# Small products of several sequences issued in turn, and copies shared out anew, in a hybrid attention step

## The chip, the cores and the metric

The kernel runs on one core of a Trainium2 chip. A core has five engines with a queue each: TensorE (PE in the profile, its weight loads PEld), VectorE (DVE), ScalarE (ACT), GpSimd (POOL) and SyncE (SP), which issues most DMAs. An engine takes the instructions of its queue in order. The metric is the device time of one execution in microseconds, lower is better.

## What is computed

One step of a hybrid decoder layer is run for a prompt of 1024 tokens and for a sample group of 8 sequences with 4 new tokens each, which share the weights. The part that matters here is the sparse attention of the sample group, for each of the two key/value heads:

```
kcmp, vcmp = compress(k), compress(v)      # 127 block summaries of the 2048 cached rows
lc  = q . kcmp * scale + bias;   pc = softmax(lc);   o_cmp = pc . vcmp
imp = pc . sel_map;              idx = top_k(imp, 16 blocks of 64 rows)
ls  = q . selected rows * scale + bias;   o_slc = softmax(ls) . selected values
lw  = q . window rows * scale + bias;     o_win = softmax(lw) . window values   # 512 rows
a   = g0 * o_cmp + g1 * o_slc + g2 * o_win
```

A summary is gelu(flat(block + pe) @ w1) @ w2, a small network over 32 rows at a stride of 16. Everything is float32. Behind the attention follow the merge with the short convolution, w_o, a residual, a squared-ReLU MLP and a final norm.

## The kernel before

Large products are split into a high and a low part in a faster float32 format (`mm3`, three products each, lines 212 to 214). The small products of the sample attention are plain float32, which the array runs as two passes each.

The work of the sample group stands beside the compression of its cache. The compression handles the 16 caches (8 sequences, keys and values): the first six key caches one at a time in `sample_unit` with `comp_unit` during the prompt's attention, and the other ten two by two in `pair_unit`. A pair unit gathers the raw rows by an indirect DMA on POOL's queue, puts them in order by heads (`by_heads`, four quarters q for each sequence; q = 3 on POOL, the others on VectorE), transposes them (ct), evicts them on ScalarE (xt), and forms three sums of products (hid), for which VectorE and ScalarE prepare the differences and the two parts (dx, cth, ctl). `blocks_out` applies the gelu and the second weights (kvc) and leaves kcT or vcN.

The sample attention is a generator, `sample_group`, and each `yield` is a place where it can be left. The loop over the pair units resumes it SSTEP = (5, 4, 4) times after the three sums of each unit; what is left runs after the loop. The order on the engines is then planned by the compiler's scheduler from this order of the program, with its own estimate of times.

`sample_group` treats two groups of four sequences. Each sequence's queries are 32 columns (2 heads, 4 query heads, 4 tokens), so a product has 32 stationary columns, and the sequence j of a group writes the PSUM rows 32j to 32j + 31. For each group, `weights`:
- loads four window keys (`swn`, two buffers) and transposes each (`flipped`: four PE transposes into one of two PSUM tiles skT, one eviction into one of five tiles skt);
- forms the products with the summaries and the new keys (sn, lines 1133 to 1135) and with the windows (sw, line 1142), the softmaxes, the importance and the choice of blocks (im, sel);
- takes, for each half of the cached rows, the four gathered tiles (`gk`, four buffers, 512 KB each, fetched by `gather_half` on POOL's queue) one sequence after another: two flips of four tiles, each followed by its product (sl, line 1192), the eviction of the first on VectorE and that of the second on ScalarE, then `fetch()` for the next gather and a yield; then the mask is added into L;
- takes the softmax, the window values (sv, line 1113), and transposes the weights in five parts, which go to DRAM (sl_d).

`values` reads them back and forms the products with the gathered values, eight for each sequence and half (so, line 1231), those with the summaries and the new values (lines 1244 and 1245), and puts the result into the rows of aT, from which the merge (na) goes on.

Of the kernel before, what the change touches and what calls it, by code (L numbers as in the profile page):

```python
# [11 lines left out]
F32 = mybir.dt.float32  # L12
# [60 lines left out]
SSTEP = (5, 4, 4)  # L73
# [46 lines left out]
def tile_hybrid_step(ctx, tc, xp, xs, cck, ccv, csk, csv, swk, swv, sconv, ptab, g_attn, w_in,  # L120
# [317 lines left out]
    kcT = mp.tile([128, NB, 127], F32, name="kcT")  # L438
# [48 lines left out]
    def blocks_out(kv, x, t, n, b):  # L487
# [11 lines left out]
        if kv == "k":  # L499
# [8 lines left out]
            else:  # L508
                for h in range(2):
                    for mt in range(2):  # L510
                        PE.matmul(po[h * 64:h * 64 + 64, :nblk], w2[:, mt, 0, :], xh[:, mt, :nblk, h],
                                  start=mt == 0, stop=mt == 1)
                V.tensor_copy(kcT[:, b, :], po[:, :nblk])
# [12 lines left out]
    def comp_unit(kv, w1, cv, n, b):  # L526
# [60 lines left out]
        x, t = (mp.tile([128, 2, 256], F32, name=nm, tag=nm, bufs=1) for nm in ("gx", "gt"))  # L587
        for mt in range(2):
            S.activation(x[:, mt, :nv], hv[:, mt, :nv], AF.Identity, bias=pb[:, mt:mt + 1])
# [39 lines left out]
    def by_heads(raw, q):  # L629
# [3 lines left out]
        if q in GPRP:  # L633
            P.tensor_scalar(dst, src, 1.0, 0.0, op0=OP.mult, op1=OP.add)
        else:
            V.tensor_copy(dst, src)
# [6 lines left out]
    def pair_unit(kv, cache, b0, w1):  # L643
# [5 lines left out]
        for q in range(4):  # L649
            xt = u2.tile([128, 2, 512], F32, name="xt", tag="xt", bufs=XTB)  # L650
            for s_ in range(2):
                part = by_heads(raws[s_], q)
# [7 lines left out]
        x = u2.tile([128, 2, 512], F32, name="gx2", tag="gx2", bufs=1)  # L660
        xo = x.rearrange("p m (j e h) -> p m j e h", e=2, h=2)
# [426 lines left out]
    CN, CC, CS = 127, 0, 131  # L1088
    new_rows = {}

    def sample_group():
# [13 lines left out]
        def window_values(pw, rows, bs, ow):  # L1105
            pt = flipped([pw[:, i * 128:(i + 1) * 128] for i in range(4)], S.copy)
            po3 = ps(HT["sx"], "sv")
            for j, b in enumerate(bs):
                nat = s1.tile([128, 4, 128], F32, name="swn", tag="swn", bufs=SWB)
                DMA.dma_start(nat, swv[0, b].rearrange("(k p) h d -> p k (h d)", p=128))  # L1110
                keep_window(s_wv[0, b], nat)
                for i in range(4):
                    PE.matmul(po3[rows[j], :128], pt[:, i * 128 + 32 * j:i * 128 + 32 * j + 32], nat[:, i, :],
                              start=i == 0, stop=i == 3)
            V.tensor_copy(ow, po3[:, :128])

        def weights(grp):
# [14 lines left out]
            for r, b in zip(rows, bs):  # L1132
                PE.matmul(po2[r, CC:CC + 127], qb[b], kcT[:, b, :], start=True, stop=True)
                PE.matmul(po2[r, CN:CN + 4], qb[b], newT[:, 1, b * 4:b * 4 + 4], start=True, stop=True)
                PE.matmul(po2[r, CS:CS + 4], qb[b], newT[:, 0, b * 4:b * 4 + 4], start=True, stop=True)
            sn = s1.tile([128, 136], F32, name="snc", tag="snc")
            V.tensor_copy(sn[:, :135], po2[:, :135])
# [3 lines left out]
            for r, b, kt in zip(rows, bs, kts):  # L1141
                PE.matmul(po[r, :], qb[b], kt, start=True, stop=True)
# [43 lines left out]
            for half in range(2):  # L1186
                pl = [ps(HT["sx"], "sl") for _ in range(2)]
                for j, b in enumerate(bs):
                    g = gathered.pop(0)
                    for l in range(2):  # L1190
                        kt = flipped([g[:, i * 128:(i + 1) * 128] for i in range(4 * l, 4 * l + 4)], (V.tensor_copy, S.copy)[l])
                        PE.matmul(pl[l][rows[j], :], qb[b], kt, start=True, stop=True)  # L1192
                    fetch()
                    yield
                for l in range(2):
                    c = slice((2 * half + l) * 512, (2 * half + l + 1) * 512)
                    V.tensor_add(L[:, c].rearrange("p (l k c) -> p l k c", l=4, c=4),
                                 pl[l].rearrange("p (l k c) -> p l k c", l=4, c=4), selb)
# [10 lines left out]
            for q in range(5):  # L1209
                kt = flipped([L[:, i * 128:(i + 1) * 128] for i in range(4 * q, 4 * q + 4)] if q < 4 else [pc_, mx],  # L1210
                             S.copy if q % 2 else V.tensor_copy)
# [4 lines left out]
        def values(grp, ow):  # L1216
# [7 lines left out]
            for half in range(2):  # L1224
                pl = [weights_T(2 * half + i, 512) for i in range(2)]
                oo = ps(HT["sx"], "so")
                for j, b in enumerate(bs):
# [618 lines left out]
```

## Time and profile before

| | us |
|---|---|
| median of 3 runs | 1945.8 (1941.43 to 1947.84) |
| the profiled execution | 1940.09 |
| its span, first to last instruction | 1938.0 |

The profile is of one execution. Its page gives the busy time of each engine over the span; further views answer by groups of instructions (line, engine, operation, tiles written and read, shape, count, then busy time and mean ns of one, then the idle time of the engine just before them and what ended it), by stretches of time, or instruction by instruction along the timeline. In a row such as `128*32 128x512`, 128 rows and 32 columns are stationary and 512 elements of 128 partitions are moved. A matmul's time runs from its start to its modelled end, which overlaps the next one's start; what a run of them costs is read from start to start.

The whole span in 40 slices of 48.45 us, for two engines, in tenths:

```profile
PE   8999999999999999989999999999999999999998
DVE  6323332445446766758877362597766655767765
```

The pair units and the sample attention lie in the slices 18 to 23, about 858 to 1102 us.

### The profile page before, as it was taken

Reading aid. Unit: us, or ns where it says so; the run is one execution under the profiler, and the core shown is the slowest. Engines: PE = TensorE matmul, PEld = TensorE weight load, DVE = VectorE, ACT = ScalarE, POOL = GpSimd, SP = SyncE. Lnnn points to the kernel's source line nnn. Section 1 sums busy time; section 2 is a strip of 40 time slices with the busy share of each in tenths; the row PEclk is TensorE's granted clock in tenths of the full one; section 3 lists DMA queues with packets and bytes.
Section 4 is the critical chain, followed back from the end, with each engine's and each line's share of the span. In section 5 each row is a group of like instructions: output and inputs, shape, how many; then the busy total and the mean of one; then the engine's idle time right before and its main releaser. Section 6 shows DMA issues by size and latency. Waiting matters only on the chain.

```text
span 1938.0 us, 34844 instructions
## 1 busy us (share of the span) xinstructions
PE 1885.6 (97%) x13172; PEld 1753.9 (91%) x13172; DVE 1132.3 (58%) x2393; ACT 857.6 (44%) x1905; POOL 412.3 (21%) x590
## 2 busy tenths in 40 slices
PE   8999999999999999989999999999999999999998
PEld 7999999999998988876769897899999999999998
DVE  6323332445446766758877362597766655767765
ACT  5112323555555555645545221465544444544333
POOL 3112223443444443423132240020000000000000
PEclk9999999999999999999999999999999999999999
DMA  6356326212226531146546654537765666765654
GB/s 213 127 146 147 97 66 160 81 58 73 71 67 206 180 109 54 48 149 208 181 136 201 208 193 134 156 103 242 235 225 192 213 243 207 251 188 162 187 193 159
DMA packets 236312, 303.77 MB, mean 157 GB/s; under 512 B 20662, under 2 KB 163143, under 8 KB 232049
## 3 DMA queue, kind: packets, MB, share of 16 engines
q1 hardware_dynamic: 229232, 267.99, 44.3%
q0 software_dynamic: 6912, 33.56, 5.1%
q8 instruction: 104, 1.70, 0.4%
q14 instruction: 64, 0.52, 0.1%
HBM read 222.78 MB, written 78.71 MB: 156 GB/s over the span
## 4 chain that ended last, share of the span: by engine, by line
PE 84%; DMA 6%; DVE 4%; issue 3%; ACT 1%; POOL 1%; SPq 1%; DVEq 0%; POOLq 0%; ACTq 0%
PE c L213 9%; PE c L212 9%; PE c L214 9%; PE PT L939 3%; PE ga L213 3%; PE ga L212 3%; PE ga L214 3%; PE hid L213 2%; PE hid L214 2%; PE hid L212 2%; DMA wrd<-sd_d 2%; PE pv L946 2%; PE pv L945 2%; PE sl L1192 2%; PE so L1231 1%
## 5 line engine op out<-in xcount | busy, mean ns | idle before, releaser
L212 PE MATMUL c<-ud,whd 128*128 128x264 f32 x768 | 217.8, 286 | 6.2 <-ACT whd L1642 4.1
L214 PE MATMUL c<-ud,whd 128*128 128x264 f32 x768 | 217.6, 286 | 0.0
L213 PE MATMUL c<-ud,whd 128*128 128x264 f32 x768 | 217.5, 285 | 0.0
L865 POOL TENSOR_SCALAR P<-P,st,gates 128x256 f32<-128x256 f32 (+4 forms) x272 | 151.5, 577 | 118.5 <-DVE st L861 96.4
L212 PEld LDWEIGHTS c<-ud,whd 128*128 128x128 f32 x768 | 144.8, 190 | 6.8 <-ACT whd L1642 4.3
L212 PE MATMUL c<-hBt,wuh 128*128 128x264 f32 x512 | 146.3, 287 | 2.4 <-ACT hBt L1553 2.4
L214 PE MATMUL c<-hBt,wul 128*128 128x264 f32 x512 | 146.3, 286 | 0.0
L213 PEld LDWEIGHTS c<-ud,whd 128*128 128x128 f32 x768 | 145.3, 190 | 0.0
L214 PEld LDWEIGHTS c<-ud,whd 128*128 128x128 f32 x768 | 144.8, 190 | 0.0
L943 DVE TENSOR_TENSOR ptl<-PT,pth 128x512 fp32r<-128x512 f32 (+1 forms) x148 | 99.5, 686 | 66.2 <-ACT pth L942 65.8
L1642 ACT CAST whd<-wrd 128x512 fp32r<-128x512 f32 x112 | 68.3, 621 | 147.4 <-issue 97.3
L212 PE MATMUL ga<-hTh,whu 128*128 128x384 f32 (+1 forms) x384 | 127.7, 333 | 0.0
L213 PE MATMUL ga<-hTl,whu 128*128 128x384 f32 (+1 forms) x384 | 126.3, 329 | 0.0
L214 PE MATMUL ga<-hTh,wlu 128*128 128x384 f32 (+1 forms) x384 | 125.9, 328 | 0.0
L235 POOL TENSOR_TENSOR wlu<-wru,whu 128x1024 fp32r<-128x1024 f32 x32 | 76.8, 2399 | 222.6 <-ACT whu L234 222.6
L1643 DVE TENSOR_TENSOR whd<-wrd,whd 128x512 fp32r<-128x512 f32 x112 | 76.4, 690 | 79.1 <-ACT whd L1642 79.0
L942 ACT CAST pth<-PT 128x512 fp32r<-128x512 f32 (+1 forms) x148 | 83.8, 589 | 66.9 <-PE PT L939 64.2
L213 PE MATMUL c<-h2r,wuh 128*128 128x264 f32 x384 | 109.4, 285 | 0.0
L213 PE MATMUL hid<-ctl,w1h 128*128 128x254 f32 (+1 forms) x352 | 103.8, 295 | 4.2 <-DVE ctl L679 4.1
L212 PE MATMUL hid<-cth,w1h 128*128 128x254 f32 (+1 forms) x352 | 101.2, 287 | 1.2 <-ACT cth L678 0.6
L939 PE MATMUL PT<-cst,P 128*128 128x128 f32 (+1 forms) x592 | 100.6, 274 | 0.8 <-POOL P L865 0.5
L212 PEld LDWEIGHTS c<-hBt,wuh 128*128 128x128 f32 x512 | 97.4, 191 | 2.9 <-ACT hBt L1553 2.6
(539 smaller groups left out, 5890.5 us busy)
## 6 DMA issues: line engine op xcount, KB each, us to landing
ur<-u_d SPq DMA_DIRECT2D x96, 264.0 KB
wru<-in_w_up SPq DMA_DIRECT2D x36, 512.0 KB
u_d<-u SPq DMA_DIRECT2D x64, 264.0 KB
wru<-in_w_in SPq DMA_DIRECT2D x32, 512.0 KB
h2r<-in_w_down SPq DMA_DIRECT2D x32, 512.0 KB
sd_d<-h2r SPq DMA_DIRECT2D x16, 1024.0 KB
wrd<-sd_d SPq DMA_DIRECT2D x64, 256.0 KB
wrd<-in_w_down SPq DMA_DIRECT2D x48, 256.0 KB
```

Of the source, the lines that this page charges most:

```text
L212: PE.matmul(out, wh, ah, start=first, stop=False)
L213: PE.matmul(out, wh, al, start=False, stop=False)
L214: PE.matmul(out, wl, ah, start=False, stop=last)
L235: (leng or P.tensor_sub)(l, raw, f32(h))
L865: P.tensor_scalar(p, p, self.st[:, br, 3, g:g + 1], gates[:, self.qi, 3 * hg + br:3 * hg + br + 1], op0=OP.mult, op1=OP.mult)
L939: PE.transpose(pt[:n, g * 128:(g + 1) * 128], pg[g], ident)
L942: S.copy(hi[:n], pt[:n])
L943: V.tensor_sub(lo[:n], pt[:n], f32(hi[:n]))
L945: PE.matmul(self.o, w, hi[:n], start=first and i == 0, stop=False)
L946: PE.matmul(self.o, w, lo[:n], start=False, stop=last and i == len(tiles) - 1)
L1642: S.copy(h, raw)
L1643: lows.append(V.tensor_sub(l, raw, f32(h)))
```

## The change

Products of four sequences (sn, sw, sl, and the last ones of the values) or of two (sv, so) are issued in turn, so that neighbouring ones write different rows of the PSUM tile. A helper, `in_turn`, issues a list of them and ties all but the first behind the first (`issue_after`: an order on the engine's queue, without a wait). The last sequence stands first in each list. For sl the loop is turned round: the four gathered tiles of a half are taken at once; for each l all four are flipped, then the four products follow. The gathers for the next half are issued with the flips of l = 1. In sv and so, two tiles are taken and then two fetched.

The evictions of flipped tiles go to ScalarE but for the first of each half and the first of the five parts of the weights. In pair units `by_heads` puts q = 1 on POOL and q = 2 on ScalarE. The summaries of the keys get a 128th column (kcT; the gelu's input is set to zero there by a memset on POOL, once for each unit), so the columns of sn move by one. In `blocks_out` the two heads alternate. SSTEP becomes (4, 4, 4).

```diff
-SSTEP = (5, 4, 4)
+SSTEP = (4, 4, 4)
...
-                for h in range(2):
-                    for mt in range(2):
-                        PE.matmul(po[h * 64:h * 64 + 64, :nblk], w2[:, mt, 0, :], xh[:, mt, :nblk, h],
+                for mt in range(2):
+                    for h in range(2):
+                        PE.matmul(po[h * 64:h * 64 + 64, :n], w2[:, mt, 0, :], xh[:, mt, :n, h],
                                   start=mt == 0, stop=mt == 1)
...
+        P.memset(x[:, :, nv:], 0.0)
...
-        if q in GPRP:
+        if q in GPRP or pair and q == 1:
             P.tensor_scalar(dst, src, 1.0, 0.0, op0=OP.mult, op1=OP.add)
+        elif pair and q == 2:
+            S.copy(dst, src)
         else:
             V.tensor_copy(dst, src)
...
+        P.memset(x[:, :, 510:], 0.0)
...
+    def in_turn(products):
+        with ExitStack() as e:
+            for i, (out, w, a, first, last) in enumerate(products):
+                ins = PE.matmul(out, w, a, start=first, stop=last)
+                if i == 0:
+                    e.enter_context(tc.issue_after(ins.ins))
...
-            for j, b in enumerate(bs):
-                nat = s1.tile([128, 4, 128], F32, name="swn", tag="swn", bufs=SWB)
-                DMA.dma_start(nat, swv[0, b].rearrange("(k p) h d -> p k (h d)", p=128))
-                keep_window(s_wv[0, b], nat)
-                for i in range(4):
-                    PE.matmul(po3[rows[j], :128], pt[:, i * 128 + 32 * j:i * 128 + 32 * j + 32], nat[:, i, :],
-                              start=i == 0, stop=i == 3)
+            for j0 in (0, 2):
+                nats = {}
+                for j in (j0, j0 + 1):
+                    nats[j] = s1.tile([128, 4, 128], F32, name="swn", tag="swn", bufs=SWB)
+                    DMA.dma_start(nats[j], swv[0, bs[j]].rearrange("(k p) h d -> p k (h d)", p=128))
+                    keep_window(s_wv[0, bs[j]], nats[j])
+                in_turn([(po3[rows[j], :128], pt[:, i * 128 + 32 * j:i * 128 + 32 * j + 32], nats[j][:, i, :], i == 0, i == 3)
+                         for i in range(4) for j in (j0 + 1, j0)])
...
-            for r, b, kt in zip(rows, bs, kts):
-                PE.matmul(po[r, :], qb[b], kt, start=True, stop=True)
+            in_turn([(po[r, :], qb[b], kt, True, True) for r, b, kt in list(zip(rows, bs, kts))[::-1]])
...
-                pl = [ps(HT["sx"], "sl") for _ in range(2)]
-                for j, b in enumerate(bs):
-                    g = gathered.pop(0)
-                    for l in range(2):
-                        kt = flipped([g[:, i * 128:(i + 1) * 128] for i in range(4 * l, 4 * l + 4)], (V.tensor_copy, S.copy)[l])
-                        PE.matmul(pl[l][rows[j], :], qb[b], kt, start=True, stop=True)
-                    fetch()
-                    yield
+                gs = [gathered.pop(0) for _ in bs]
                 for l in range(2):
+                    kts = []
+                    for j, g in enumerate(gs):
+                        kts.append(flipped([g[:, i * 128:(i + 1) * 128] for i in range(4 * l, 4 * l + 4)],
+                                           V.tensor_copy if l + j == 0 else S.copy))
+                        if l:
+                            fetch()
+                        if j == 1:
+                            yield
+                    pl = ps(HT["sx"], "sl")
+                    in_turn([(pl[r, :], qb[b], kt, True, True) for r, b, kt in list(zip(rows, bs, kts))[::-1]])
                     c = slice((2 * half + l) * 512, (2 * half + l + 1) * 512)
                     V.tensor_add(L[:, c].rearrange("p (l k c) -> p l k c", l=4, c=4),
-                                 pl[l].rearrange("p (l k c) -> p l k c", l=4, c=4), selb)
+                                 pl.rearrange("p (l k c) -> p l k c", l=4, c=4), selb)
+                    yield
...
-                             S.copy if q % 2 else V.tensor_copy)
+                             S.copy if q else V.tensor_copy)
...
-                for j, b in enumerate(bs):
-                    g = gathered.pop(0)
-                    for i in range(8):
-                        c = i % 4 * 128 + 32 * j
-                        PE.matmul(oo[rows[j], :128], pl[i // 4][:, c:c + 32], g[:, i * 128:(i + 1) * 128],
-                                  start=i == 0, stop=i == 7)
-                    fetch()
+                for j0 in (0, 2):
+                    gs = {j: gathered.pop(0) for j in (j0, j0 + 1)}
+                    in_turn([(oo[rows[j], :128], pl[i // 4][:, i % 4 * 128 + 32 * j:i % 4 * 128 + 32 * j + 32],
+                              gs[j][:, i * 128:(i + 1) * 128], i == 0, i == 7) for i in range(8) for j in (j0 + 1, j0)])
+                    for _ in gs:
+                        fetch()
                     yield
```

The products of sn and those with the summaries and the new values (lines 1244 and 1245) are put into `in_turn` in the same way, all long ones ahead of all short ones.

More of the change, by code (lines that the diff above doesn't have):

```diff
@@ L437, in tile_hybrid_step @@
     mp = open_pool("cmp", "left")
-    kcT = mp.tile([128, NB, 127], F32, name="kcT")
+    kcT = mp.tile([128, NB, 128], F32, name="kcT")
     vcN = mp.tile([127, NB, 128], F32, name="vcN")
@@ L508, in blocks_out @@
             else:
-                for h in range(2):
-                    for mt in range(2):
-                        PE.matmul(po[h * 64:h * 64 + 64, :nblk], w2[:, mt, 0, :], xh[:, mt, :nblk, h],
+                for mt in range(2):
+                    for h in range(2):
+                        PE.matmul(po[h * 64:h * 64 + 64, :n], w2[:, mt, 0, :], xh[:, mt, :n, h],
                                   start=mt == 0, stop=mt == 1)
-                V.tensor_copy(kcT[:, b, :], po[:, :nblk])
+                V.tensor_copy(kcT[:, b, :], po[:, :n])
         else:
@@ L627, in gather, with by_heads @@
         return g
-    def by_heads(raw, q):
+    def by_heads(raw, q, pair=False):
         by_head = up.tile([128, 2, 256], F32, name="gpr", tag="gpr", bufs=2)
@@ L651, in pair_unit @@
             for s_ in range(2):
-                part = by_heads(raws[s_], q)
+                part = by_heads(raws[s_], q, True)
                 pt = ps(HT["ct"], "ct")
@@ L1086, in keep_window @@
         DMA.dma_start(dst[:128 - ST].rearrange("p h d -> p (h d)"), rows[ST:, 0])
-    CN, CC, CS = 127, 0, 131
+    CN, CC, CS = 128, 0, 132
+    def in_turn(products):
[4 more added lines that the diff above has]
+                    e.enter_context(tc.issue_after(ins.ins))
     new_rows = {}
@@ L1131, in weights @@
             po2 = ps(HT["sx"], "sn")
[L1132 to L1135, printed above, removed]
+            back = list(zip(rows, bs))[::-1]
+            in_turn([(po2[r, CC:CC + 128], qb[b], kcT[:, b, :], True, True) for r, b in back] +
+                    [(po2[r, c:c + 4], qb[b], newT[:, br, b * 4:b * 4 + 4], True, True)
+                     for c, br in ((CN, 1), (CS, 0)) for r, b in back])
             sn = s1.tile([128, 136], F32, name="snc", tag="snc")
-            V.tensor_copy(sn[:, :135], po2[:, :135])
+            V.tensor_copy(sn, po2[:, :136])
             V.tensor_add(sn[:, CC + 119:CC + 127], sn[:, CC + 119:CC + 127], sb_b[:, 15:128:16])
@@ L1242, in values @@
             oo = ps(HT["sx"], "so")
-            for j, b in enumerate(bs):
-                PE.matmul(oo[rows[j], :128], pl[:127, rows[j]], vcN[:, b, :], start=True, stop=False)
-                PE.matmul(oo[rows[j], :128], pl[:8, 128 + 32 * j:160 + 32 * j], vn[:, j, :], start=False, stop=True)
+            back = list(enumerate(bs))[::-1]
+            in_turn([(oo[rows[j], :128], pl[:127, rows[j]], vcN[:, b, :], True, False) for j, b in back] +
+                    [(oo[rows[j], :128], pl[:8, 128 + 32 * j:160 + 32 * j], vn[:, j, :], False, True) for j, b in back])
             V.tensor_add(ow, ow, oo[:, :128])
```

## The prediction

> **What bounds the kernel now.** I read the page first, then the busy time of the engines by stretches, then the instruction groups of the stretch in which the change lies, and last the timeline of single spots.
>
> ```profile
> span 1938.0 us, 34844 instructions
> PE 1885.6 (97%) x13172; PEld 1753.9 (91%) x13172; DVE 1132.3 (58%) x2393; ACT 857.6 (44%) x1905; POOL 412.3 (21%) x590
> ```
>
> TensorE is busy for 97% of the span, so time comes off where TensorE gets less to do, as long as nothing else then takes over. All products that the change re-orders lie between 858 and 1102 us. The stretches, from the view of busy time by windows:
>
> ```profile
> 858.00:945.00 87.00, 79.12 (x546) 57.24 (x547) 69.23 (x148) 46.09 (x93) 22.23 (x20) 0.96 0.61 190
> 945.00:1045.00 100.00, 100.00 (x717) 79.98 (x715) 79.06 (x140) 53.98 (x98) 23.95 (x22) 1.00 0.49 156
> 1045.00:1102.00 57.00, 56.92 (x450) 49.35 (x449) 21.73 (x46) 11.53 (x21) 15.84 (x16) 1.00 0.76 257
> ```
>
> The columns after the length are PE, PEld, DVE, ACT and POOL, then clock, DMA share and GB/s. I call the rows A, B and C. PE has 7.9 us of idle in A, none in B, 0.1 in C. VectorE is the next engine: 80% in A, 79% in B, 38% in C. In C the DMA queues are 76% busy. The groups of this stretch:
>
> ```profile
> L1192 PE MATMUL sl<-skt,qbd 128*32 128x512 f32 x64 | 31.2, 604 | 0.0
> L1231 PE MATMUL so<-gk,skt 128*32 128x128 f32 x256 | 28.7, 274 | 0.0
> L1142 PE MATMUL sw<-skt,qbd 128*32 128x512 f32 x16 | 8.4, 605 | 0.0
> L1113 PE MATMUL sv<-swn,skt 128*32 128x128 f32 x64 | 6.6, 276 | 0.2 <-DMA swn<-in_state_win_v 0.2
> L1244 PE MATMUL so<-vcN,skt 127*32 127x128 f32 x16 | 3.2, 283 | 0.0
> L1245 PE MATMUL so<-skt 8*32 8x128 f32 x16 | 3.2, 280 | 0.0
> L511 PE MATMUL kvc<-gx,w2k 128*64 128x127 f32 x24 | 2.0, 287 | 0.0
> ```
>
> The program has 32 sl products and the trace 64 instructions: each float32 product is two passes. All have 32 stationary columns, a quarter of the array (L511: 64).
>
> **Does the array run columns side by side?** The trace already has the answer, since the scheduler once put three sl products of three sequences together:
>
> ```profile
> 902.88 0.28 PE L213 MATMUL hid<-ctl,w1h 128*128 128x254 f32 x1
> 903.00 0.28 PE L214 MATMUL hid<-cth,w1l 128*128 128x254 f32 x1
> 903.21 1.06 PE L1192 MATMUL sl<-skt,qbd 128*32 128x512 f32 x6
> 904.20 0.55 PE L1100 MATMUL skT<-cst,gk 128*128 128x128 f32 x3
> 904.68 1.04 PE L1192 MATMUL sl<-skt,qbd 128*32 128x512 f32 x2
> 905.66 0.33 PE L1100 MATMUL skT<-cst,gk 128*128 128x128 f32 x1
> ```
>
> Six passes (three products) take from 903.21 to 904.20, 0.99 us; two passes (one product) from 904.68 to 905.66, 0.98 us. Three cost what one costs. Entering such a run costs about 0.09 us more (903.00 to 903.21 against the 0.12 from 902.88 to 903.00). Products of one column after each other do not overlap:
>
> ```profile
> 1044.93 0.28 PE L212 MATMUL hid<-cth,w1h 128*128 128x256 f32 x1
> 1045.14 5.95 PE L1231 MATMUL so<-gk,skt 128*32 128x128 f32 x64
> 1051.02 0.33 PE L517 MATMUL kvc<-w2v,gx 128*127 128x64 f32 x1
> ...
> 1066.20 1.94 PE L1231 MATMUL so<-gk,skt 128*32 128x128 f32 x16
> 1068.06 0.38 PE L212 MATMUL hid<-cth,w1h 128*128 128x254 f32 x1
> ```
>
> One sequence's sixteen so passes take 1.86 us; four sequences in a row take 5.88 us instead of 7.44, so a little of the neighbouring columns overlaps at the three borders between sequences, 0.5 us each. A column takes its passes one after another, and the engine looks only a few passes ahead for another column. Issued in turn, two columns should therefore always be fed.
>
> The Trainium skill, page "TensorE: Matmul & The Clock Gate", section "The mechanism", says that a weight load overlaps a matmul in flight only where the row group differs; here all columns use all rows, so by that rule the change would gain little (the second rival). The rows at 903.21 speak against it. The same page ("Measured speedup vs the span model") gives 2.38 times for three columns; by that a set of four would cost at least 1.23 us instead of 0.99, ten sets 2.4 us more than below. The trace has 2.97 times (three times 0.98 by 0.99), and the measurement decides.
>
> **The change part by part.** TensorE, busy time before and after:
> - sl: 31.2 us before. Now 8 sets (2 groups, 2 halves, 2 values of l) of four columns. Four at once the trace doesn't show: at best they cost what three do, 1.06 us busy, at worst the fourth stands alone, 0.98 more. I take 1.06, the nearest row: 8 x 1.06 = 8.5, saving 22.7.
> - sw: 8.4 before, now two such sets, 2.1, saving 6.3.
> - so (selected values): 28.7 before; now 8 pairs, each pair in the time of one sequence, 1.94: 15.5, saving 13.2.
> - sv: 6.6; four pairs of eight passes a column, 1.94 less 8 x 0.11 = 1.06 each: 4.2, saving 2.4.
> - L1244 and L1245: 6.4; two sets, each one long and one short product (about 0.4 each): 1.6, saving 4.8.
> - sn (L1133 to L1135), from the timeline:
>
> ```profile
> 862.42 0.63 PE L1133 MATMUL sn<-kcT,qbd 128*32 128x127 f32 x2
> ...
> 864.44 0.48 PE L1100 MATMUL skT<-cst,swn 128*128 128x128 f32 x1
> ...
> 931.38 0.40 PE L1133 MATMUL sn<-kcT,qbd 128*32 128x127 f32 x2
> ...
> 932.56 0.39 PE L214 MATMUL hid<-cth,w2l 128*128 128x256 f32 x1
> ```
>
> The first group's 24 passes take 2.02 us, the second's 1.18. I estimate about 0.6 for each afterwards (a kcT row's 0.40 and a few short passes), saving 2.0. The kvc products (L511) already overlap at the border of their two columns; with three runs of 0.6 us here I count nothing.
>
> Sum: 22.7 + 6.3 + 13.2 + 2.4 + 4.8 + 2.0 = 51.4 us: 17 in A, 16.4 in B, 18 in C. If the fourth column stood alone in all ten sets, it would be 41.6.
>
> The copies that are shared out anew, and the gathers (groups, then the DMA view with the time from issue to landing in us):
>
> ```profile
> L1102 ACT COPY skt<-skT 128x512 f32<-128x512 f32 x30 | 17.6, 588 | 29.2 <-PE skT L1100 28.7 <-PE hid L214 0.2
> L1102 DVE COPY skt<-skT 128x512 f32<-128x512 f32 x20 | 13.7, 686 | 7.2 <-PE skT L1100 6.8
> L636 DVE COPY gpr<-gth 128x512 f32<-128x512 f32 x28 | 11.9, 425 | 3.5 <-DMA gth<-in_cache_cmp_v,idx 1.2 <-PE hid L214 1.1 <-PE ct L657 1.0
> L634 POOL TENSOR_SCALAR gpr<-gth 128x512 f32<-128x512 f32 x10 | 9.0, 908 | 39.6 <-PE ct L657 39.0 <-DVE w1l L480 0.6
> L618 POOL DMA_INDIRECT gk<-in_cache_slc_v,idx x16 | 16.7, 1041 | 58.9 <-PE so L1231 44.2 <-PE skT L1100 8.7 <-DVE L L1197 5.4
> ```
>
> ```profile
> gk<-in_cache_slc_v,idx POOLq DMA_INDIRECT x16, 5.9
> ```
>
> - Evictions of transposed keys: per group 6 of 8 leave VectorE for ScalarE (only the one with l + j = 0 stays), and 2 of 3 evictions of the weights. Over both groups VectorE loses 16 x 0.686 = 11 us, ScalarE gains 16 x 0.588 = 9.4.
> - by_heads in the five pair units: 10 copies (q = 1) go to POOL, 10 (q = 2) to ScalarE. VectorE loses 20 x 0.425 = 8.5, POOL gains 10 x 0.9 = 9, ScalarE about 10 x 0.59.
> - Shares afterwards, stretches shortened by the sums above: VectorE in A 69.2 less 7.5 (6 evictions, 8 copies) = 61.7 of 70, 88%; in B 79.1 less 11.9 (6 + 4 evictions, 12 copies) = 67.2 of 83.7, 80%. ScalarE in A 46.1 + 5.9 = 52 of 70, 74%; in B 54.0 + 9.4 = 63.4 of 83.7, 76% (54% before).
> - POOL also gets 13 small memsets. The nearest row is the memset of 128x64; the row after it, of the groups between 858 and 1102, is TensorE's wait for ctl, used below:
>
> ```profile
> L903 POOL MEMSET P<- 128x64 f32 x12 | 1.8, 152 | 37.1 <-PE PT L939 36.9
> ```
>
> ```profile
> L213 PEld LDWEIGHTS hid<-ctl,w1h 128*128 128x128 f32 x160 | 30.2, 188 | 5.8 <-DVE ctl L679 5.4 <-DVE stt L1078 0.2 <-issue 0.2
> ```
>
> About 2 us on an engine that is 75% idle: nothing, unless a memset waits for its buffer with a gather behind it on POOL's queue; at the 6.9 us of a gather for each of the five pair units that would be 35, at the other end 0. I take 0, since POOL's gathers are issued long ahead (58.9 us of idle before them).
> - Waits that the change adds: the first product of a set is the last sequence's, so it waits for the last eviction, and the hid products behind it on PE's queue wait with it. The four gathered tiles of a half (GK = 4) are held until the flips for l = 1, so the next half's gathers go out later; in values two gathers go out after each pair. SWB = 2 windows are now used as a pair, so two loads start together afterwards; PE idled 0.2 us for them before, I take 0.
> - Steps: the sample group needs 54 resumes instead of 62, and 60 are given instead of 65, so it runs ahead of the units rather than behind them.
>
> What is late next: in A it is VectorE (PE already waits 5.4 us for ctl), I take 3 us; in B ScalarE, 3 us; in C the DMA queues, 0.76 x 57 = 43.3 us of work against 39 left for PE, 4.3 us. Sum 10. **Gain 51 - 10 = 41 us.** The profiled execution took 1940.1 (span 1938.0), 5.7 below the median 1945.8; taking 41 off the median gives 1904.8.
>
> **The rivals.**
> 1. *Evictions pace the sets.* Four flips take PE some 0.44 us, their evictions on ScalarE 4 x 0.588 = 2.35, and the set waits for the last. With no hid product between, each of ten sets loses up to 1.9 + 0.6 = 2.5 us: 25 of the 51 are gone, gain 26, 1920. For it: ScalarE now evicts nearly all, with two PSUM banks (sk). Against it: it idled 28.7 us waiting for PE, and there is hid work to put between. The Trainium skill, "TensorEngine Tiling (Array Packing)", section "PSUM Bottleneck", names this danger; no row of before shows it yet.
> 2. *The columns don't overlap as meant* (weights wait for the column in flight). Two sl products that ran one behind the other:
>
> ```profile
> 1014.93 1.90 PE L1192 MATMUL sl<-skt,qbd 128*32 128x512 f32 x4
> 1016.76 0.33 PE L1100 MATMUL skT<-cst,pw 128*128 128x128 f32 x1
> ```
>
> They take 1.83 us, so the second costs 0.85 where one alone costs 0.98 + 0.09. Only this 0.22 goes, for each of some 26 runs of sl and sw, and about half of the 4.8 of L1244 and L1245: 8 us, 1938. Against it the row at 903.21.
> 3. *Slower: gathers are exposed.* A gather takes 1.04 + 5.9 = 6.9 us. If PE has nothing to put there, three changes of half cost 6.9 each, and six of the eight value pairs wait for two gathers less the other pair's run, 2 x 1.04 + 5.9 - 1.94 = 6.0 each: 20.7 + 36 = 57 us, more than 51, so 6 slower: 1951. It decides the sign once the nine waits average over 51.4 / 9 = 5.7 us. Against it: PE idled 0.0 before so, and POOL waited 44.2 us for PE rather than PE for POOL.
>
> **How the numbers follow.** Forecast (gain 33 to 60, 1886 to 1913): 0.63. Rival 1 or a mixture of it with the fourth column alone (gain 14 to 33, 1913 to 1932): 0.23. Rival 2: 0.05. Rival 3: 0.05. A larger gain, if the relief of VectorE also removes idle of A: 0.04. The range 1886 to 1932 holds the first two, 0.86, which I count as 8 in 10 since a re-planned order may shift any of them. Faster by over 0.3% (5.8 us, about what a measurement of this kernel can tell from no change): 0.63 + 0.23 + 0.04 and half of rival 2, 0.92; within: 0.03; slower: 0.05.
>
> **What would show it.** Right: sl rows of eight passes that take about 1 us, PE busy on sl near 8.5 and on so near 16, the stretch from the first sn to the last so about 200 us instead of 240. Rival 1 would show as idle of PE or a late sl behind ACT skt; rival 2 as sl sets of 3.5 us; rival 3 as idle of PE released by DMA gk. The forecast fails if TensorE gets less to do but idles as much more, or if the new order delays the weights that later stages load.

## The result, and the profile after

| | before | after |
|---|---|---|
| median of 4 runs, us | 1944.47 (1941.43 to 1947.84) | 1915.72 (1908.89 to 1917.36) |
| ratio, 95% interval | 1 | 0.9845 [0.9815, 0.9875] |
| profiled execution, us | 1940.09 | 1917.36 |

The change takes 28.8 us off the median; the two executions that were profiled lie 22.7 apart, as that of before is 4.4 below its median and that of after, the longest of its four, 1.6 above. The forecast was 1904.8 with a range of 1886 to 1932: direction and range held, the gain was 12 us smaller than forecast. The page of after begins:

```profile
span 1915.4 us, 34882 instructions
...
PE 1850.2 (97%) x13172; PEld 1745.0 (91%) x13172; DVE 1117.3 (58%) x2357; ACT 869.3 (45%) x1931; POOL 423.8 (22%) x613
```

TensorE lost 35 us of busy time, and the span only 23. The busy time of the engines of after in the stretches A, B and C (columns as in the prediction):

```profile
858.00:945.00 87.00, 72.34 (x570) 63.08 (x571) 65.80 (x127) 55.59 (x110) 26.47 (x27) 0.84 0.56 178
945.00:1045.00 100.00, 95.23 (x889) 86.59 (x889) 75.86 (x140) 59.92 (x116) 35.14 (x38) 1.00 0.66 215
1045.00:1102.00 57.00, 47.84 (x374) 44.92 (x373) 33.51 (x65) 18.66 (x37) 16.85 (x16) 0.91 0.73 255
```

Two things are new. TensorE idles 14.7 us in A, 4.8 in B and 9.2 in C, where it idled 7.9, none and 0.1 (C now holds more of the merge, since the sample products end sooner). And the granted clock, 0.96 and 1.00 before, is 0.84 in A and 0.91 in C. The products themselves, in the groups of after from 858 to 1102 us (all now carry L1100, the line of the helper `in_turn`):

```profile
L1100 PE MATMUL so<-gk,skt 128*32 128x128 f32 x256 | 15.5, 280 | 3.8 <-DMA gk<-in_cache_slc_v,idx 3.8
...
L1100 PE MATMUL sl<-skt,qbd 128*32 128x512 f32 x64 | 8.5, 605 | 0.0
...
L1100 PE MATMUL sv<-swn,skt 128*32 128x128 f32 x64 | 4.2, 274 | 0.6 <-DMA swn<-in_state_win_v 0.6
...
L1100 PE MATMUL sw<-skt,qbd 128*32 128x512 f32 x16 | 2.1, 604 | 0.0
...
L1100 PE MATMUL so<-vcN,skt 127*32 127x128 f32 x16 | 1.2, 282 | 0.0
L1100 PE MATMUL sn<-kcT,qbd 128*32 128x128 f32 x16 | 1.1, 353 | 0.0
L1100 PE MATMUL sn<-newT,qbd 128*32 128x4 f32 x32 | 1.1, 189 | 0.0
L1100 PE MATMUL so<-skt 8*32 8x128 f32 x16 | 0.8, 280 | 0.0
```

The same numbers of instructions, each as long as before (sl 605 ns against 604), but with overlaps counted once 32.9 us of busy time in all instead of 82.9. One set of four columns and one pair, from the timeline of TensorE of after:

```profile
977.96 1.06 PE L1100 MATMUL sl<-skt,qbd 128*32 128x512 f32 x8
978.95 0.66 PE L1115 MATMUL skT<-cst,gk 128*128 128x128 f32 x4
...
1057.86 1.94 PE L1100 MATMUL so<-gk,skt 128*32 128x128 f32 x32
1059.73 1.16 PE L518 MATMUL kvc<-w2v,gx 128*127 128x64 f32 x8
```

Eight passes take from 977.96 to 978.95, 0.99 us, what one product took alone (0.98); thirty-two passes of a pair take 1.87 us, what sixteen took (1.86). So the overlap is complete with two columns and with four.

**Where the 48 us went.** For the table below each product of TensorE was charged the time from its start to the next start, less what lies past its own end, which is idle; the stage runs from the first ct product after 700 us to the first wo product. Half clock is time in which the granted clock is 0.5. All in us:

```
kernel                  stage   narrow   wide, full clock   wide, half clock   idle   time at half clock
before                  441.4     79.1              334.7                8.8   18.8                 13.7
whole change            415.1     31.4              318.2               33.1   32.3                 44.4
four columns only       428.2     49.7              323.3               25.2   30.1                 34.1
pairs only              433.2     60.4              330.4               15.4   26.9                 27.3
first sequence first    433.0     60.7              328.1               20.9   23.3                 30.7
filler in the gap       411.7     33.8              335.1               14.4   28.4                 27.3
one more buffer         409.6     33.9              328.5               15.7   31.5                 20.5
buffer, weight earlier  402.0     32.2              328.9               15.0   25.9                 17.1
```

"Narrow" are sn, sw, sl, sv and so, "wide" all other products; the lower rows are experiments below. Between before and the whole change narrow products fall by 47.7. Idle takes back 13.5. The wide products cost 7.8 more: if those at half clock take twice their time, they cost 16.5 more than at full clock instead of 4.4, 12.1 us, while the wide work itself is 4.4 us less at full clock. Twice is a little too much: the hid products of after start 0.213 us apart at half clock and 0.119 at full (medians), 1.8 times, and by that the clock costs 10.7 and the wide work is 2.9 less. I put the latter to the runs of narrow products being fewer, 22 instead of 55, each of which cost 0.09 us to enter, 3.0 in all, but no run shows it by itself. (The wide products of the filler run hold the 4.7 us of the filler.) So the stage is 26.3 shorter. (It starts 1.8 later and what follows it is 1.9 longer in this execution: 22.6 of span.)

These two executions overstate the clock's share. Over the whole span their granted clocks are 0.992 and 0.983, while 46 timed runs of before lie between 0.985 and 0.992, 0.989 in the mean, and the four of after between 0.983 and 0.988, 0.985 in the mean. A clock lower by 0.001 is 3.9 us more at half clock in such a span, so in the mean the change adds some 14 us at half clock and not the 34 of these two (31 of them in the stage), which by the same reckoning costs 6 to 7 us. That would account for most of the 6 us by which the medians lie further apart than the two executions.

The idle has names. TensorE's waits of before (838 to 1118 us; total, times, longest in us):

```profile
PE ct L657 <- DVE kcT L513: 6.2, 1, 6.2
PE hid L213 <- DVE ctl L679: 4.1, 6, 1.1
PE na L212 <- ACT wnh L1302: 3.1, 1, 3.1
```

and of after (838 to 1100 us):

```profile
PE ct L661 <- DVE kcT L514: 5.2, 1, 5.2
PE hid L213 <- DVE ctl L684: 4.8, 3, 3.5
PE na L212 <- ACT wnh L1320: 4.6, 1, 4.6
PE hid L212 <- ACT cth L683: 3.8, 3, 2.5
PE so L1100 <- DMA gk<-in_cache_slc_v,idx: 3.8, 2, 3.3
PE skT L1115 <- DMA swn<-in_state_win_k: 1.8, 2, 0.9
PE ct L661 <- POOL gpr L636: 1.7, 2, 1.4
PE skT L1115 <- ACT skt L1117: 1.7, 1, 1.7
```

The largest wait was there before. It is for a copy queued on VectorE behind weights that are still being loaded, as VectorE's timeline of after shows:

```profile
861.46 0.43 DVE L473 TENSOR_TENSOR both<-w1r 128x256 f32<-128x256 f32 x1 [0.89 <-DMA w1r<-in_cmp_w_k]
861.80 0.28 DVE L514 COPY kcT<-kvc 128x128 f32<-128x128 f32 x1
```

The waits for the last weights of the merge (wnh) and for ctl were there too and are longer one by one. New, or a few tenths before, are those on ScalarE (cth 3.8, skt 1.7), the gathers (3.8), the windows (1.8) and POOL (1.7). The units and the sample group share TensorE; as the group's share went from 79 to 31 us, the units' operands and the gathers have that much less time to come.

How one such wait becomes two losses, from TensorE's timeline of after (the number in brackets is idle before the instruction):

```profile
905.31 0.66 PE L1115 MATMUL skT<-cst,gk 128*128 128x128 f32 x4
909.42 0.58 PE L213 MATMUL hid<-ctl,w2h 128*128 128x256 f32 x1 [3.45 <-DVE ctl L684]
909.80 0.42 PE L214 MATMUL hid<-cth,w2l 128*128 128x256 f32 x1
910.02 0.41 PE L212 MATMUL hid<-cth,w2h 128*128 128x256 f32 x1
```

After 3.45 us of idle the hid products start 0.22 us apart (909.80, 910.02) instead of the 0.12 of the prediction's rows. The stretches at half clock of after last 3.4, 3.4, 13.7, 6.8, 6.8, 3.4 and 6.8 us, multiples of 3.4. The Trainium skill, "TensorE: Matmul & The Clock Gate", section "What's actually happening", gives that unit: a window of about 3.4 us, idle in one halving the clock and busy in one restoring it. The lengths agree. But a window here need not be idle throughout: in the 3.4 us before the half clock that begins at 907.5 TensorE idled 1.8 us, and before that of 842.6 only 1.0. Other such stretches with up to 1.5 us of idle were followed by none.

### The profile page after: what moved, and what is told of

Same layout as the page of the kernel before. It is cut to its first block, busy times and chain, and to the rows that moved or that the text cites. A ratio compares the mean times of both kernels' runs of the same rounds, so it can differ in the third digit from the quotient of the medians.

```text
span 1915.4 us, 34882 instructions
## 1 busy us (share of the span) xinstructions
PE 1850.2 (97%) x13172; PEld 1745.0 (91%) x13172; DVE 1117.3 (58%) x2357; ACT 869.3 (45%) x1931; POOL 423.8 (22%) x613
## 5 line engine op out<-in xcount | busy, mean ns | idle before, releaser
L214 PE MATMUL hid<-cth,w1l 128*128 128x254 f32 (+1 forms) x352 | 100.5, 286 | 0.0
```

Source lines behind the costliest of these rows:

```text
L214: PE.matmul(out, wl, ah, start=False, stop=last)
```

## The experiments

Every run was timed beside the kernel before on the same chip; the ratio is to that. e1 to e4 shared one set of runs before (1944.44), e5 to e7 one (1943.72), e8 to e10 one (1947.88), e11 and e12 one (1943.01). Since the medians before differ by up to 5 us, kernels of different calls are compared by ratio, or by what each gains on its own before. The diffs are against the kernel after, unless they say otherwise.

**Which part carries the gain.** e1: the new order with the old sharing of copies and evictions.

```diff
-                part = by_heads(raws[s_], q, True)
+                part = by_heads(raws[s_], q)
-                                           V.tensor_copy if l + j == 0 else S.copy))
+                                           (V.tensor_copy, S.copy)[l]))
-                             S.copy if q else V.tensor_copy)
+                             S.copy if q % 2 else V.tensor_copy)
```

> The order of the products as changed, the copies and evictions shared as before the change. Theory (the order alone takes 47 us of narrow products off TensorE, and VectorE's load sets how much comes back as idle): VectorE keeps 20 us of copies that the change takes away, so idle and half clock grow further; 1918 to 1930, a gain of 15 to 27. Rival (the copies now on ScalarE and POOL are what TensorE waits for): 1900 to 1912, better than the whole change.

Measured: 1921.8 us, 0.9890 [0.9870, 0.9910], 22.6 us gained.

e2: the reverse, the kernel before with those three lines (and `by_heads`) as they are after; this diff is against before.

```diff
-                part = by_heads(raws[s_], q)
+                part = by_heads(raws[s_], q, True)
-                        kt = flipped([g[:, i * 128:(i + 1) * 128] for i in range(4 * l, 4 * l + 4)], (V.tensor_copy, S.copy)[l])
+                        kt = flipped([g[:, i * 128:(i + 1) * 128] for i in range(4 * l, 4 * l + 4)], V.tensor_copy if l + j == 0 else S.copy)
-                             S.copy if q % 2 else V.tensor_copy)
+                             S.copy if q else V.tensor_copy)
```

> The copies and evictions shared as after the change, the order of the products as before. Theory (TensorE is the bound, it idled only some 19 us between 704 and 1145 us): 1938 to 1948, within 0.3% of before. Rival (VectorE is a second bound already before): a gain of 8 us or more, under 1936.

Measured: 1943.87 us, 0.9999 [0.9987, 1.0011]. Sharing the copies anew brings nothing as long as the order is the old one. With the new order it is the difference between e1 and the whole change, about 6 us by medians and 9 by ratios, with intervals that overlap a little.

e3: four columns (sn, sw, sl) as after; the products of sv, of so and the last ones as before.

```diff
-                    in_turn([(oo[rows[j], :128], pl[i // 4][:, i % 4 * 128 + 32 * j:i % 4 * 128 + 32 * j + 32],
-                              gs[j][:, i * 128:(i + 1) * 128], i == 0, i == 7) for i in range(8) for j in (j0 + 1, j0)])
...
+                for j, b in enumerate(bs):
+                    g = gathered.pop(0)
+                    for i in range(8):
...
```

> The whole change but for the products with window and selected values and the last ones of the values (sv, so, lines 1244 and 1245 of before), which stand as before. Theory (each part gives back its own share): TensorE's time for sl, sw and sn falls by 28 as in the whole change, that for so and sv stays near 39; the gain is about 6 tenths of 28, 1922 to 1932. Rival (the sets of four bring the stalls, since they wait for four evictions and hold four gathered tiles): a gain under 10, over 1935.

Measured: 1929.66 us, 0.9930 [0.9912, 0.9948], 14.8 us gained with 29.4 us of narrow products saved in the table.

e4: so, sv, the last products and sn as after; sw and sl one by one as before.

```diff
-            in_turn([(po[r, :], qb[b], kt, True, True) for r, b, kt in list(zip(rows, bs, kts))[::-1]])
+            for r, b, kt in zip(rows, bs, kts):
+                PE.matmul(po[r, :], qb[b], kt, start=True, stop=True)
...
+                    for l in range(2):
...
+                        PE.matmul(pl[l][rows[j], :], qb[b], kt, start=True, stop=True)
```

> The whole change but for the products with window keys and selected keys (sw, sl), which stand as before, one sequence after another, with the evictions shared as changed. Theory: so, sv and the last products take 19 us less of TensorE as in the whole change; 1926 to 1936. Rival (the values wait for gathers, so their gain is lost again): over 1938.

Measured: 1937.36 us, 0.9962 [0.9947, 0.9976]: 7.1 us gained with 18.7 saved, a little less than the least that was expected. In both halves, and in the whole, about four to six tenths of what TensorE saves reaches the time (14.8 of 29.4, 7.1 of 18.7, 28.8 of 47.7). So the loss is not the fault of one kind of set alone.

**Copies and evictions one by one.** e5: the second copy by heads back on VectorE. e10: the evictions back as before, the copies by heads as after.

```diff
-        if q in GPRP or pair and q == 1:
+        if q in GPRP:
```

> The whole change, but the copies by heads of q = 1 stay on VectorE as before the change (q = 2 still goes to ScalarE). Theory (POOL's stretch of work from 904.6 to 908.3 held one VectorE instruction for 4.27 us, which made TensorE idle for 3.45 us and dropped its clock for 6.8 us): that stall goes, 1908 to 1913 against 1915.7 for the whole change. Rival (VectorE's load is what counts, 10 more copies of 0.43 us): 1916 to 1922.

Measured: 1917.29 us, 0.9877 [0.9859, 0.9895]. No gain, although the hold of 4.27 us that was expected to go is gone (no VectorE instruction takes over 2.4 us in the stage of e5) and the longest wait for ctl falls from 3.5 to 2.4 us: that one stall is not what costs the time.

```diff
-                                           V.tensor_copy if l + j == 0 else S.copy))
+                                           (V.tensor_copy, S.copy)[l]))
-                             S.copy if q else V.tensor_copy)
+                             S.copy if q % 2 else V.tensor_copy)
```

> The whole change, but evictions of transposed keys and weights shared as before the change (l = 0 on VectorE, l = 1 on ScalarE; the weights in turn), the copies by heads as changed. Theory (with copies and evictions both as before, 6 us were lost; with q = 1 alone 1.6): evictions hold most of it, 1918 to 1923. Rival (evictions on one engine pace the sets, two engines are better): 1905 to 1913.

Measured: 1916.03 us, 0.9841 [0.9817, 0.9865], the ratio of the whole change, so the loss that was expected did not come. ScalarE as the one that evicts is neither gain nor loss. This speaks against rival 1 of the prediction: with half of the evictions taken off ScalarE the time stays.

**Does the order within a set matter?** e6: the same sets, first sequence first.

```diff
-            back = list(zip(rows, bs))[::-1]
+            back = list(zip(rows, bs))
-                         for i in range(4) for j in (j0 + 1, j0)])
+                         for i in range(4) for j in (j0, j0 + 1)])
...
```

> The whole change, but each list of products stands in the order of the sequences, the first one first. Theory: the columns overlap as well, but the first product is now free to go before the last eviction, so TensorE then stands in order before the later ones and has nothing behind them to do; more idle before sl and so, 1920 to 1935. Rival (the planner leaves the set until all is ready anyway): 1911 to 1920.

Measured: 1936.15 us, 0.9966 [0.9952, 0.9980]. Of the 28.8 us some 20 are gone, a little more than expected, and by another way than a wait. TensorE's timeline of e6 shows how:

```profile
915.30 1.04 PE L1100 MATMUL sl<-skt,qbd 128*32 128x512 f32 x2
916.28 0.39 PE L212 MATMUL hid<-cth,w2h 128*128 128x256 f32 x1
916.59 0.68 PE L512 MATMUL kvc<-gx,w2k 128*64 128x128 f32 x8
917.20 1.05 PE L1100 MATMUL sl<-skt,qbd 128*32 128x512 f32 x2
```

The four products of a set stand apart again, each of its own 0.98 us. As I read these rows, the planner places a product when its keys are ready and puts other work in between; with the first product waiting for the last keys, the other three are ready behind it and stay together. The groups of e6 say the same: sl 30.3 us of busy time as before, while the pairs of so, whose operands come together, stay at 16.1:

```profile
L1100 PE MATMUL sl<-skt,qbd 128*32 128x512 f32 x64 | 30.3, 604 | 0.0
...
L1100 PE MATMUL so<-gk,skt 128*32 128x128 f32 x256 | 16.1, 275 | 3.4 <-DMA gk<-in_cache_slc_v,idx 3.4
```

**The idle and the clock.** e7: 24 products without use, meant for the 5.2 us gap at 857 to 862.

```diff
+    idle, fill = ps("lg", "idle"), cst.bitcast(BF16)[:, :512]
+    for _ in range(24):
+        PE.matmul(idle, fill[:, :128], fill, start=True, stop=True)
```

> The whole change, and 24 bfloat16 products of 512 columns (some 5 us, result unused) where TensorE waits at the change of pools, near 857 us. Theory (idle costs twice, the second time as half clock: 13.7 us of half clock follow this gap): the gap stays, the half clock behind it goes or shrinks, 1908 to 1913. Rival (at half clock TensorE was waiting for copies anyway): 1914 to 1920, no gain.

Measured: 1920.31 us, 0.9894 [0.9877, 0.9912]. Inconclusive: the planner put them at 815 us, ahead of the gap, where they cost their own time.

e9: 22 such products tied behind the kvc products that end before the gap.

```diff
+                        kvc_last[b] = PE.matmul(po[h * 64:h * 64 + 64, :n], w2[:, mt, 0, :], xh[:, mt, :n, h],
...
+    with tc.issue_after(kvc_last[ATTEND - 1].ins):
+        for _ in range(22):
+            PE.matmul(idle, fill[:, :128], fill, start=True, stop=True)
```

> The whole change, and 22 bfloat16 products of 512 columns (4.8 us, result unused) tied behind the kvc products after which TensorE waits some 5 us near 857 us. The filler of the run before had been planned at 815 us, so it cost its own 5 us and tells nothing of the gap. Theory (idle costs a second time as half clock, 13.7 us of it behind this gap): the gap is filled at no cost, the half clock behind it goes or shrinks by half, 1908 to 1913. Rival (at half clock TensorE waits for copies anyway): 1914 to 1919.

Measured: 1914.48 us, 0.9825 [0.9803, 0.9846]. TensorE's timeline of e9 has the filler in its place:

```profile
856.23 4.70 PE L1344 MATMUL idle<-cst 128*128 128x512 bf16 x21 [0.16 <-issue]
862.35 1.09 PE L662 MATMUL ct<-cst,gpr 128*128 128x128 f32 x8 [1.42 <-DVE kcT L515]
```

and its windows a clock of 0.96 in A instead of 0.84:

```profile
858.00:945.00 87.00, 76.62 (x630) 62.93 (x629) 69.48 (x144) 58.86 (x120) 31.20 (x31) 0.96 0.64 204
```

17 us less at half clock, but the stage is only 3.4 us shorter and the time the same within its interval. Behind the gap half clock falls from 13.7 to 6.8 us, but from 1066 on it rises from 10.2 to 17.1, where TensorE now waits 3.3 us for a gather, 3.6 for a copy of VectorE and 2.6 for the merge's weights. Nor is all of the 17 the filler's doing: e7, whose gap stands as before, has only 23.9 us at half clock in the stage, so the same gap can be followed by more or less of it. Over the runs the clock of e9 is 0.988 in the mean against 0.985, some 11 us less at half clock, which would be worth about 5; the ratios differ by 3.9 us, with intervals that overlap. So the price of the clock is neither shown nor refuted by this run.

e8: the copy behind which the gap stands waits on VectorE behind weights that come late, as only two raw tiles are in flight; a third tile lets them load earlier.

```diff
-            raw = w1p.tile([128, 2, 256], F32, name="w1r", tag="w1r", bufs=2)
+            raw = w1p.tile([128, 2, 256], F32, name="w1r", tag="w1r", bufs=3)
```

> The whole change, and three buffers instead of two for the raw first weights (w1r). Theory (between 845 and 925 us VectorE and ScalarE stand in order before weight loads that wait for one of two buffers, and TensorE waits for the copies behind them): the idle of TensorE in that stretch falls by 5 or more and with it the half clock, 1903 to 1911 against 1915.7. Rival (the loads wait for the DMA queues, not for a buffer): 1912 to 1919.

Measured: 1914.24 us, 0.9830 [0.9808, 0.9853], not to be told from the whole change. The gap itself falls from 5.2 to 0.4 us, and idle in the table only from 32.3 to 31.5, though half clock from 44.4 to 20.5. The first waits in the list of e8 (838 to 1100 us) are now late ones, for the last weights of the merge and for the last gathers:

```profile
PE na L212 <- ACT wnh L1320: 4.8, 2, 4.5
PE so L1100 <- DMA gk<-in_cache_slc_v,idx: 3.5, 1, 3.5
```

e11: that buffer, and the third piece of the merge's weights asked for ahead of the merge's own loads.

```diff
-            raw = w1p.tile([128, 2, 256], F32, name="w1r", tag="w1r", bufs=2)
+            raw = w1p.tile([128, 2, 256], F32, name="w1r", tag="w1r", bufs=3)
-    merge = [load_merge(j) for j in range(MJ)]
-    wns.append(load_wn(2))
+    wns.append(load_wn(2))
+    merge = [load_merge(j) for j in range(MJ)]
```

> The whole change, three buffers for the raw first weights as in the run before, and the load of the third merge weight (wnr) ahead of the merge inputs (ta, cg) instead of behind them. Theory (behind the last value products TensorE waits 4.6 us for this weight, which stands behind 3.2 MB of merge inputs in the DMA queues): that wait falls by 3 or more, 1906 to 1911 by the scale of the runs where the whole change took 1915.7. Rival (the weight is late for a place on ScalarE's queue): 1912 to 1917.

Measured: 1908.92 us (1902.10 to 1910.13), 0.9811 [0.9788, 0.9835]: the fastest kernel measured here, and clearly faster than before. Against the whole change it is 6.8 us by medians, with ratios whose intervals overlap from 0.9815 to 0.9835. TensorE's waits of e11 (838 to 1100 us) begin at a lower size:

```profile
PE skT L1115 <- DMA gk<-in_cache_slc_k,idx: 3.1, 4, 1.3
PE hid L214 <- DVE w2l L475: 2.3, 1, 2.3
PE na L213 <- DVE aTl L1385: 2.2, 1, 2.2
```

No single wait is above 2.3 us, 17 us are at half clock instead of 44, and the stage takes 402.0 us instead of 415.1. One wait removed (e8, e9) brought nothing that could be measured; two removed together brought some 5 to 7 us, not quite clear of the noise. The earlier load was not tried alone.

e12: is it the amount of DMA? The copies of kept window rows (16 transfers of 192 KB) are left out, so those rows of two outputs are not written.

```diff
-        DMA.dma_start(dst[128 - ST:WIN - ST].rearrange("(k p) h d -> p k (h d)", p=128), rows[:, 1:])
```

> The whole change without the 16 larger DMAs that write the kept window rows out (192 KB each, 3.1 MB; those rows of two outputs stay unwritten). Theory (from 858 us on the sample stretch is now partly paced by DMAs: weights, windows, gathers): 1905 to 1911, 5 or more faster. Rival (the copies on VectorE and ScalarE pace it, the DMAs fit beside them): 1912 to 1918, no change.

Measured: 1912.85 us, 0.9845 [0.9825, 0.9864], the ratio of the whole change. These copies do not pace it. They are all issued before 1013 us, and in C the queues of this run are 77% busy against 73% in after, so it says nothing of the loads of the merge that go there.

## Why the prediction was right in its sign and too large in its size

- **That columns run side by side** (first step, rows at 903.21 and 1045.14): right, and rival 2 falls. Four at once were not in the trace of before; the bound that was taken, the price of three, is what they cost (0.99 us). By the 2.38 times for three columns of the Trainium skill ("TensorE: Matmul & The Clock Gate", section "Measured speedup vs the span model") a set would have cost an estimated 1.23 at least; measured are four for 0.99, nearly 4 times.
- **The sum of TensorE's work**, 51.4: right within 4 us. Busy time fell by 50.0, start to start by 47.7. Term by term: sl 8.5 (predicted 8.5), so 15.5 (15.5), sw 2.1 (2.1), sv 4.2 (4.2), the last products 2.0 (1.6), sn 1.8 busy and 1.4 start to start (1.2).
- **What is late next**, 10: this is the step that failed, by size. It had idle of VectorE, ScalarE and DMA at 3 + 3 + 4.3 us; the idle that came is 13.5, and by that alone the time would have been 3.5 us off. What it lacked is a term for the clock: 44 us at half instead of 14 in the two traces, worth 11 to 12, and in the mean of the runs 6 to 7. The prediction read the granted clock of A, 0.96, without asking what more idle would do to it. With the 4.4 less of wide work that it didn't count either, 47.7 + 4.4 - 13.5 - 12.1 gives 26.5, the 26.3 of the stage but for rounding. Of the 15 us between these 26.3 and the 41.4 that were forecast, 3.7 are the sum's, 3.5 the idle's and 12.1 the clock's, less the 4.4.
- **The range** held partly by luck. 1915.7 lies outside the 1886 to 1913 of the forecast itself, in the band that was given 0.23 for rival 1 or a fourth column that stands alone, and the traces show neither.
- **Why those waits**: the directions were right in kind but not one by one. VectorE in A was put at 88% of the shortened stretch; its 3.5 us wait for ctl came not from load but from a single instruction that was held (last section). ScalarE shows as 3.8 us for cth, of which 3.2 in A and not in B. The merge's weights, which the prediction named only among what would make it fail, are 4.6 instead of 3.1.
- **Rival 1**, evictions: at 1920 it lies nearer to the result than the forecast, but its mechanism is hardly there. TensorE waits 1.7 us for ACT skt in all, instead of 0.4, and e10 leaves the time unchanged. Its price was worked out wrongly as well: 0.44 us is one flip of four transposes, so four take 1.76, and the excess would have been some 1.2 us a set and not 2.5. The Trainium skill's "PSUM Bottleneck" ("TensorEngine Tiling (Array Packing)"), weighed there, finds hardly any support in these runs.
- **Rival 3**, gathers exposed: the mechanism exists, at a fifteenth of its price. TensorE and POOL of after at the last half of the values:

```profile
1066.31 0.42 PE L1100 MATMUL so<-skt 8*32 8x128 f32 x8
1070.07 2.49 PE L1100 MATMUL so<-gk,skt 128*32 128x128 f32 x32 [3.34 <-DMA gk<-in_cache_slc_v,idx]
```

```profile
1060.07 0.94 POOL L620 DMA_INDIRECT gk<-in_cache_slc_v,idx  x1 [5.04 <-PE so L1100]
1061.31 1.31 POOL L620 DMA_INDIRECT gk<-in_cache_slc_v,idx  x1 [0.30 <-issue]
```

  The last two gathers go out together after a pair (POOL waited 5.04 us for it), and the pair that needs them waits 3.34 us. That is once in the trace, and 3.8 us in all instead of 57, and not at every change. The argument that gathers go out long ahead misread its row: the 58.9 us are idle of POOL that mostly ended with TensorE (so 44.2), so POOL waited for tiles to come free and gathered as soon as they did.
- **The shares of copies** were costed as part of the loss. Measured, they are worth nothing alone (e2) and some 6 us with the new order (e1 against the whole). Taking back one part shows no clear loss: e10 none; e5 2 us by medians and 6 by ratios, with an interval that overlaps both that of e1 and that of the whole. The copies of q = 2 were not taken back alone. Which part makes the 6 us is open.
- **The signs** came as named: sl rows of eight passes near 1 us, first sn to last so from 864.0 to 1072.1, 208 us. And the case named for failure, that TensorE "idles as much more", came true in part: 13.5 of 47.7 came back as idle.

**What stays open.** The clock's price is worked out from traces, for these two executions 11 to 12 us, and not shown by a run: e9 had 17 us less at half clock and gained no more than its interval can tell. The new SSTEP, the alternating heads in `blocks_out` and the memsets came with the new order in every run and were not tried alone. Whether the merge's loads, which go through the queues in C, delay the last gathers was not tried. What paces e8 and e9 after their gap is closed was not settled beyond the waits listed; only e11 shows that the loss can be had back, in part, just within the noise and with two causes at once.

## What to carry to other kernels

Look in the trace for products of few columns that already stand side by side by chance: their start times say what grouping will bring, and here the sum came true within 4 us. Group them so that the product whose operand comes last is issued first, or a planner pulls the set apart (20 of 28.8 us). And when the busiest engine is relieved in a stage where its suppliers are busy too, do not count on all of it: here 29 of 48 us reached the time. List the supplier of each kind of operand, price the idle, and then price the clock that idle costs.

## What the runs showed of the hardware that was not expected

A VectorE instruction of 0.41 us took 4.27. VectorE and POOL of after, on the same times:

```profile
904.36 4.27 DVE L475 TENSOR_TENSOR w2l<-both,w2h 128x256 fp32r<-128x256 f32 x1
908.55 0.22 DVE L1165 TENSOR_SCALAR mx<-pw,stt 128x4 f32<-128x4 f32 x1
908.69 0.68 DVE L684 TENSOR_TENSOR ctl<-xt,cth 128x512 fp32r<-128x512 f32 x1
```

```profile
904.62 1.91 POOL L1192 TENSOR_TENSOR L<-L,lt 128x900 f32<-128x900 f32 x1
906.48 1.21 POOL L636 TENSOR_SCALAR gpr<-gth 128x512 f32<-128x512 f32 x2
907.67 0.68 POOL L1166 TENSOR_SCALAR pw<-pw,stt 128x512 f32<-128x512 f32 x1
```

VectorE's instruction ends at 908.63, just after POOL's unbroken run of 904.62 to 908.35, and the ctl that TensorE waits for comes behind it. The Trainium skill, "SBUF — State Buffer", section "SBUF: two separate sides", has a rule that fits: VectorE and GpSimd (POOL here) share a pair of ports that one of them holds for a whole instruction, and a VectorE instruction with two SBUF inputs, as this one, needs it against one of POOL that reads SBUF. The trace agrees in the main: between 700 and 1140 us after has 156 such instructions of VectorE (both, w1l, w2l, dx, ctl, wnl, wol); all 134 that met no POOL instruction at their start or 0.3 us behind it took their usual time, and of the other 22 eleven took over 0.25 us more. Two things differ from the rule's wording here: VectorE's instruction started 0.26 us ahead of POOL's, and it was held over four of them and not one (spans on POOL are rough). That the ports are the cause was not tried. It is not new with the change: in the trace of before a ctl at 878.4 us took 2.40. e5, which takes ten copies off POOL, lost the long hold and gained nothing measurable, so what such holds cost in time is open; but an idle POOL is not by itself a free place for work, as the prediction took it to be.
